# Moving operands kept even columns first and read by TensorE as two halves in turn

## The chip, the core and the metric

The kernel runs on one core of one Trainium2 chip. The metric is the device time of one execution in microseconds (us), smaller being better. The engines of the core are called TensorE (PE, matmuls; PEld, its weight loads), VectorE (DVE), ScalarE (ACT), GpSimd (POOL) and SyncE (SP). SyncE and GpSimd issue the transfers.

## What is computed

One layer on 512 tokens of width 1024: a gated feed-forward block, a token mixer, a second gated block, and a last norm.

```python
for layer in range(DEPTH):                      # DEPTH = 1
    x = x + 0.5 * swiglu(rmsnorm(x, ffn1_norm[layer]), w_gate, w_up, w_down)
    x = x + token_mixer(rmsnorm(x, mix_norm[layer]), w_in, w_out, ...)
    x = x + 0.5 * swiglu(rmsnorm(x, ffn2_norm[layer]), ...)
return rmsnorm(x, final_norm)

def swiglu(x, w_gate, w_up, w_down):            # 1024 -> 2816 -> 1024
    return (silu(x @ w_gate) * (x @ w_up)) @ w_down
```

The mixer projects to queries, keys and values (`h @ w_in`), runs four heads of differential attention (difference of two softmaxes, then a norm) and eight heads of dilated attention in three window configurations, and projects back (`mixed @ w_out`). Everything is float32.

## The kernel before

**Layout.** Activations lie transposed: 128 features on the partitions, the 512 tokens along the free axis. x is eight such tiles of 128 x 512. In most products the weights are the stationary operand (128 x 128) and an activation tile is the moving one, with 512 columns (a whole tile) or 256 (half the tokens, HS = 256).

**Three matmuls for one.** TensorE is fed with the type F32R. Each operand is split in a high part (a cast to F32R, by ScalarE) and a rest (value minus cast, by VectorE), and a product is the sum of three matmuls, in `mm3` (L140 to L143): high weights by high activations, high by rest, rest by high. So there is for each moving operand one cast and one rest: `split_x` (L148) and `early_high`/`early_low` (L1553, L1556) for the inputs of the feed-forward blocks, `activated` (L232) and `kept` (L548, its `cast` L554 and `rest` L557) for the hidden activations, `normed_x` (L257) with `t_sums`, `t_casts`, `t_rests` for the normed x and its sums, `to_mixer` (L882) for the mixer's input, `finish`, `finish_low`, `join` and `mixed_t` for the attention's output.

**The stages.** Each feed-forward block (`ffn`, L216) first does some of its hidden tiles in pairs of gate and up (8 mm3 of 512 columns each, L729), and the rest by a seven-product scheme: two output tiles by two halves of the tokens by the two halves of the inner dimension take seven products instead of eight, on sums and differences of blocks (SEVEN, L46; `product`, L463), 256 columns each, four mm3 per product. The moving operands of a product are picked by `moving` (L426) from the halves of xh/xl or from the sums th/tl. Of the down projection six hidden tiles are done plainly (512 columns, L471), the rest by seven products. The mixer computes queries and keys by mm3 of 512 columns (`qk_chunks`, L1006), scaled copies `scaled` (L1025) bring them from PSUM to SBUF, and values with the activation as the stationary operand and the weights as the moving one (`v_chunks`, L967, L985 to L987). Scores (L1196, L1197), transposes (L1220, L1320) and values by probabilities (L1237, L1339) follow. The output projection does four tiles plainly (`wo_mm`, L1419, 512 columns) and four by seven products (`product`, L1510, from `mixed`).

**Order.** TensorE's order is written out by hand, and from the seventh pair on that of VectorE, ScalarE, SyncE and GpSimd too: events have planned times in ns (STEP and PLAIN_STEP, L56) and ranks, and are issued in that order. The engines then run as their semaphores let them; the planned times themselves set nothing but the order.

**Other streams named later.** `spread` (L208) multiplies ones by a diagonal tile in plain F32 to spread a factor over the partitions (bc_n, 512 columns, L210).

Of the kernel before, what the change touches and what calls it, by code (L numbers as in the profile page):

```python
# [82 lines left out]
def tile_macaron(ctx: ExitStack, tc, xs, xT, wf, wgu1, wst1, wd1, wdg1, wqk, wv, wo, wgu2, wst2, wd2,  # L83
# [15 lines left out]

    def mm_bank(nm):  # L100
        return pp.tile([P, S], F32, tag="mm", name=nm, bufs=4)
# [46 lines left out]
    def split_x(k, norm, h, l, both=False):  # L148
        g = gain(norm, k)
        if both:  # L150
            A.activation(h[:, :256], x[k][:, :256], AF.Copy, scale=g)
            V.tensor_scalar_mul(h[:, 256:], x[k][:, 256:], g)
# [63 lines left out]
    def ffn(wgu, wst, wd, wdg, n0, n1, norm, early, res, nm, hooks, ended, first=None,  # L216
# [15 lines left out]
        def activated(j, t):  # L232
            h = ah[j] = slot(j, f"ah{nm}{j}", F32R)
            l = al[j] = slot(JF + j, f"al{nm}{j}", F32R)
            parts = (lambda: A.copy(h[:], t[:]),
                     lambda: V.tensor_tensor(l[:], t[:], h[:].bitcast(F32), op=ALU.subtract))
# [38 lines left out]
        def t_sums(p, i, q):  # L275

            if not th:
                t_places()
            t0, t1 = nx[2 * p], nx[2 * p + 1]
            u0, u1 = slice(0, HS), slice(HS, S)  # L280
            if i == 0:
                o, a, b = ((t0[:, u0], t0[:, u0], t0[:, u1]), (t0[:, u1], t1[:, u1], t0[:, u1]))[q]
                V.tensor_tensor(o, a, b, op=ALU.subtract)
            else:
                o, a, b = ((t1[:, u1], t1[:, u1], t0[:, u0]), (t1[:, u0], t1[:, u1], t1[:, u0]))[q]
                V.scalar_tensor_tensor(o, a, -1.0, b, op0=ALU.mult, op1=ALU.subtract)

        def t_casts(p, i):
            t = nx[2 * p + i]
            u0, u1 = slice(0, HS), slice(HS, S)  # L290
            if p < 3:
                A.copy(th[p][:, i * S:(i + 1) * S], t[:])
            else:
                for q, u in enumerate((u0, u1)):
                    A.copy(th[p][2 * i + q], t[:, u])

        def t_rests(p, i):
# [4 lines left out]
            else:  # L302
                for q in range(2):
                    V.tensor_tensor(tl[p][:, i * S + q * HS:i * S + (q + 1) * HS],
                                    t[:, q * HS:(q + 1) * HS],
                                    th[p][2 * i + q].bitcast(F32), op=ALU.subtract)
# [119 lines left out]
        def moving(u, block):  # L426
# [7 lines left out]
            c = slice(i * HS, (i + 1) * HS)  # L434
            return [(th[p][i] if p == 3 else th[p][:, c], tl[p][:, c]) for p in range(4)]
# [27 lines left out]
        def product(t):  # L463
            u, o = ops[t]
            h, l = made.pop(t)
            if o[0] == "p":
                m = u[1]
                po = mm_bank(f"pd{nm}{m}")
                for k in range(PLAIN):
                    c = slice(k * P, (k + 1) * P)  # L470
                    mm3(po[:], h[:, c], l[:, c], ah[k][:], al[k][:], k == 0, k == PLAIN - 1)  # L471
# [9 lines left out]
            if t == 0 or ops[t - 1][1][0] == "p":  # L481
                T.matmul(banks[o[1]][:, :P], h[:, :P], moving(u, o[2])[0][0][:, :P],
# [65 lines left out]
        def kept(j, t1, t0, t2):  # L548
# [5 lines left out]
            def cast(o, a):  # L554
                A.copy(o, a)

            def rest(o, a, h):  # L557
                V.tensor_tensor(o, a, h.bitcast(F32), op=ALU.subtract)
# [15 lines left out]
            def b11():  # L574
                t["b"] = places[0]()
                A.copy(t["b"][:, left], g0[:, left])

            def b2():
                t["h2"] = places[1]()
                A.copy(t["h2"][:], g1[:])  # L580
# [5 lines left out]
            def t0_parts():  # L586
                t["h0"] = places[3]()
                A.copy(t["h0"][:], g0[:])
# [5 lines left out]
            def t1_parts():  # L594
                t["h1"] = places[5]()
                A.copy(t["h1"][:], g1[:])

            def t1_rest():
                t["l1"] = places[6]()
                rest(t["l1"][:], g1[:], t["h1"][:])  # L600
                b = hs[j] = {"b11": (t["b"][:, left], t["b"][:, right])}
                for n, i, c in (("b21", 2, left), ("b22", 2, right), ("t1", 0, left),
                                ("t3", 0, right), ("t4", 1, left), ("t2", 1, right)):
                    b[n] = t[f"h{i}"][:, c], t[f"l{i}"][:, c]
# [102 lines left out]
        for j in range(j0, n1):  # L707
# [12 lines left out]
            for hf in range(2):  # L720
# [4 lines left out]
                for kk in range(4):  # L725
                    k = hf * 4 + kk
                    for c, pt in ((0, pg), (1, pu)):
                        o = kk * 256 + c * P
                        mm3(pt[:], wh[:, o:o + P], wl[:, o:o + P], mv[0][k][:], mv[1][k][:],  # L729
                            k == 0, k == KD - 1)  # L730
# [30 lines left out]
    with tc.manual_schedule(engines={mybir.EngineType.DVE, mybir.EngineType.Activation}):  # L761
        for t in range(4):
            raw = wp.tile([P, 1024], F32, tag="raw", name=f"raw_f{t}")
            h, l = w_place()
            for kk in range(2):
# [18 lines left out]
                for j in range(2):  # L784
                    for c in range(2):
                        o = kk * 512 + (2 * j + c) * P
                        mm3(heads[j][c][:], h[:, o:o + P], l[:, o:o + P],
                            early[0][k][:], early[1][k][:], k == 0, k == KD - 1)
# [217 lines left out]
    def qk_chunks(u):  # L1006
# [3 lines left out]
        def chunk(k):  # L1010
# [14 lines left out]
        def scaled():  # L1025
            tq = st["tq"] = slot(28, f"tq{u}")
            tk = st["tk"] = slot(30, f"tk{u}")
            V.scalar_tensor_tensor(tq[:], st["pq"][:], -(HD ** -0.5), held["bc"][:],
                                   op0=ALU.mult, op1=ALU.mult)
            V.tensor_tensor(tk[:], st["pk"][:], held["bc"][:], op=ALU.mult)  # L1030
# [91 lines left out]
    def mixed_t(p):  # L1122
# [3 lines left out]
        n1 = whole["ps"] if p == 3 else t1  # L1126
        u0, u1 = slice(0, HS), slice(HS, S)
# [7 lines left out]
        steps = [lambda: less(t0[:, u0], t0[:, u0], t0[:, u1]),  # L1135
                 lambda: less(t0[:, u1], n1[:, u1], t0[:, u1]),
                 lambda: negative(t1[:, u1], n1[:, u1], t0[:, u0]),
                 lambda: negative(t1[:, u0], t1[:, u1], n1[:, u0])]

        def place():  # L1140
# [8 lines left out]
            b = mixed[p] = {"b11": (mh[2 * p][:, u0], ml[2 * p][:, u0])}  # L1149
            for n, u in (("b21", u0), ("b22", u1)):  # L1150
                b[n] = mh[2 * p + 1][:, u], ml[2 * p + 1][:, u]
            for n, i, u in (("t1", 0, u0), ("t3", 0, u1), ("t4", 1, u0), ("t2", 1, u1)):
                b[n] = o[i][:, u], o[2 + i][:, u]
# [22 lines left out]
    def attention(u, s):  # L1176
# [93 lines left out]
        def finish():  # L1270
# [5 lines left out]
            if diff:  # L1276
                A.activation(h[:], ot[:], AF.Copy, scale=sub8[:])
            else:
                A.copy(h[:], ot[:])
# [571 lines left out]
```

## Time and profile before

| What | Value |
|---|---|
| median of 3 runs | 912.99 us (912.82 to 913.25) |
| span of the profiled execution, first to last instruction | 911.9 us |
| that execution's own time | no other than the span is given; the median is 1.1 us above it |
| TensorE | busy 901.5 us, 6561 matmuls |
| weight loads | busy 844.8 us |
| VectorE, ScalarE, GpSimd | busy 759.5, 546.3, 111.2 us |
| mean granted TensorE clock | 0.996 |
| transfers | 146.86 MB, mean 161 GB/s |

A line such as `L558 DVE TENSOR_TENSOR h2a<-g1a,h1a 128x512 fp32r<-128x512 f32 x8 | 5.5, 684 | 0.0` is read so: source line, engine, operation, the tile written and the tiles read, their shapes and types, how often; then the busy time of the group in us and the mean time of one in ns; then the time that the engine sat idle just before them, and what ended it. TensorE's matmuls are pipelined, so that one's duration (276 ns for 256 columns) is longer than the distance to the next; the pace is read from the distances between starts. The granted clock is a share of TensorE's full speed.

### The profile page before, as it was taken

What the parts mean: (1) busy time and instruction counts of PE and PEld (TensorE: products, weight loads), DVE (VectorE), ACT (ScalarE), POOL (GpSimd) and SP (SyncE); (2) the same over time, 40 slices, a digit from 0 to 9 for tenths busy, and PEclk for the clock granted to TensorE, in tenths of its full rate; (3) what the DMA queues carried; (4) which work ended last, traced back from release to release, by engine and by line L of the source; (5) the groups of instructions that cost most, each with busy time, mean ns of one, the idle gap of its engine ahead of it and who ended that gap; (6) DMA issues with size and microseconds to landing.
All of it is one profiled execution on the core that took longest, in us unless ns stands there. A gap on an engine that the chain in (4) does not pass through costs nothing.

```text
span 911.9 us, 17679 instructions
## 1 busy us (share of the span) xinstructions
PE 901.5 (99%) x6561; PEld 844.8 (93%) x6561; DVE 759.5 (83%) x1603; ACT 546.3 (60%) x1152; POOL 111.2 (12%) x140
## 2 busy tenths in 40 slices
PE   9999999999999999999999999999999999999996
PEld 7889999999999998988989889889999899999995
DVE  7699997687998994788987859999899678799787
ACT  7356674355665764666756848466666354666453
POOL 1001101112203100000000220011110102220100
PEclk9999999999999999999999999999999999999998
DMA  8446756578857742345365674646784757884752
GB/s 276 116 158 155 173 141 179 139 198 216 197 146 198 218 130 92 116 128 152 104 166 146 178 142 110 173 149 154 173 201 107 196 160 180 214 222 122 188 135 93
DMA packets 66374, 146.86 MB, mean 161 GB/s; under 512 B 7680, under 2 KB 9984, under 8 KB 66288
## 3 DMA queue, kind: packets, MB, share of 16 engines
q1 hardware_dynamic: 48672, 113.29, 38.6%
q0 software_dynamic: 17616, 32.45, 21.9%
q8 instruction: 51, 0.84, 0.4%
q14 instruction: 35, 0.29, 0.1%
HBM read 137.28 MB, written 2.14 MB: 153 GB/s over the span
## 4 chain that ended last, share of the span: by engine, by line
PE 95%; DVE 3%; ACT 1%; issue 0%; DMA 0%; DVEq 0%; ACTq 0%
PE po L1237 2%; PE pv L985 2%; PE pv L987 2%; PE pv L986 2%; PE pq L141 1%; PE pq L142 1%; PE pq L143 1%; PE pk L141 1%; PE pk L143 1%; PE pk L142 1%; PE pga L141 1%; PE pga L142 1%; PE pga L143 1%; PE pua L142 1%; PE pua L141 1%; PE pua L143 1%
## 5 line engine op out<-in xcount | busy, mean ns | idle before, releaser
L1202 ACT ACTIVATE pr<-pr,small 128x128 f32<-128x128 f32 (+3 forms) x64 | 35.8, 560 | 30.8 <-DVE small L1199 30.4
L420 ACT CAST w<-s2b 128x512 fp32r<-128x512 f32 x52 | 32.3, 624 | 22.1 <-DVE s2b L402 21.8
L420 ACT CAST w<-s2a 128x512 fp32r<-128x512 f32 x48 | 29.9, 624 | 22.6 <-DVE s2a L402 21.9
L1199 DVE CUSTOM_DVE_ANT_0 pr<-sc,strip 128x128 f32<-128x128 f32 (+3 forms) x64 | 29.7, 486 | 11.5 <-PE sc L1197 11.4
L424 DVE TENSOR_TENSOR w<-s2b,w 128x512 fp32r<-128x512 f32 x52 | 35.7, 686 | 1.7 <-ACT w L420 1.1
L985 PE MATMUL pv<-w,xh 128*128 128x256 f32 x128 | 36.4, 284 | 0.0
L986 PE MATMUL pv<-w,xl 128*128 128x256 f32 x128 | 35.8, 279 | 0.0
L987 PE MATMUL pv<-w,xh 128*128 128x256 f32 x128 | 35.7, 279 | 0.0
L424 DVE TENSOR_TENSOR w<-s2a,w 128x512 fp32r<-128x512 f32 x48 | 32.9, 685 | 1.1 <-ACT w L420 0.7
L141 PE MATMUL pq<-xh,w 128*128 128x512 f32 x64 | 26.9, 421 | 0.0
L920 DVE TENSOR_TENSOR w<-raw_qk,w 128x512 fp32r<-128x512 f32 x32 | 21.6, 685 | 6.1 <-ACT w L916 6.0
L141 PE MATMUL pk<-xh,w 128*128 128x512 f32 x64 | 25.1, 393 | 0.0
L142 PE MATMUL pq<-xl,w 128*128 128x512 f32 x64 | 25.1, 392 | 0.0
L143 PE MATMUL pq<-xh,w 128*128 128x512 f32 x64 | 25.1, 391 | 0.0
L143 PE MATMUL pk<-xh,w 128*128 128x512 f32 x64 | 25.0, 391 | 0.0
L142 PE MATMUL pk<-xl,w 128*128 128x512 f32 x64 | 25.0, 391 | 0.0
L986 PEld LDWEIGHTS pv<-w,xl 128*128 128x128 f32 x128 | 24.1, 189 | 0.1
L985 PEld LDWEIGHTS pv<-w,xh 128*128 128x128 f32 x128 | 24.1, 188 | 0.2
L987 PEld LDWEIGHTS pv<-w,xh 128*128 128x128 f32 x128 | 24.1, 188 | 0.0
L916 ACT CAST w<-raw_qk 128x512 fp32r<-128x512 f32 x32 | 19.3, 616 | 7.4 <-issue 4.4
L1237 PEld LDWEIGHTS po<-v,ptb 128*128 128x128 f32 x160 | 21.6, 191 | 1.6
L1196 PE MATMUL sc<-k,q 128*128 128x256 f32 (+2 forms) x64 | 22.2, 352 | 0.2
(841 smaller groups left out, 4093.3 us busy)
## 6 DMA issues: line engine op xcount, KB each, us to landing
raw_qk<-wqk_dram SPq DMA_DIRECT2D x16, 512.0 KB, 3.7
raw0bg<-wst_dram SPq DMA_DIRECT2D x9, 512.0 KB, 4.3
raw0bu<-wst_dram SPq DMA_DIRECT2D x9, 512.0 KB, 6.0
raw_gua<-wgu_dram SPq DMA_DIRECT2D x8, 512.0 KB, 3.7
raw0ag<-wst_dram SPq DMA_DIRECT2D x8, 512.0 KB, 4.4
raw0au<-wst_dram SPq DMA_DIRECT2D x8, 512.0 KB, 5.3
raw0ad<-wdg_dram SPq DMA_DIRECT2D x8, 512.0 KB, 5.4
strip<-bias_rows SPq DMA_DIRECT2D x16, 256.0 KB, 4.1
```

The lines of the kernel that those rows point to most:

```text
L141: T.matmul(po, wh, mh, start=first, stop=False, skip_group_check=on)
L142: T.matmul(po, wh, ml, start=False, stop=False, skip_group_check=on)
L143: T.matmul(po, wl, mh, start=False, stop=last, skip_group_check=on)
L420: A.copy(made[t][0], source(t))
L424: V.tensor_tensor(l, source(t), h.bitcast(F32), op=ALU.subtract)
L985: T.matmul(po, xh[k][:, xs], wh[:, o:o + 256], start=k == 0, stop=False)
L986: T.matmul(po, xl[k][:, xs], wh[:, o:o + 256], start=False, stop=False)
L987: T.matmul(po, xh[k][:, xs], wl[:, o:o + 256], start=False, stop=k == KD - 1)
L1196: T.matmul(ps[:, :n], qs[:, qi], ks[:, :n], start=True, stop=False)
L1199: V.tensor_tensor_reduce(out=pi, in0=ps[:, :w], in1=st["b"][m][:, w - 1::-1], op0=ALU.add, op1=ALU.min, scale=1.0, scalar=3.0e38, accum_ou ...
L1202: A.activation(pi, pi, AF.Exp, scale=-1.0, bias=st["mx"][:, m, i:i + 1], accum_out=st["ls"][:, m, i:i + 1])
L1237: T.matmul(st["po3"][:, i, d0:d0 + dn], st["ptb", m, i][:, k * P:(k + 1) * P], vk, start=k == 0, stop=k == i)
```

## The change

Helpers for access patterns are added. `evens` reads a row of columns as (even ones, odd ones), that is with a step of two elements; `flat` writes these two halves one behind the other; `full` reads such a tile back in the natural order, column 0 from the first half, column 1 from the second and so on, so its inner dimension has 2 elements, 256 apart for a tile of 512 columns. `part_of` does that for the first or second 256 tokens, `side` names the columns of one half of the tokens without turning them.

```diff
+    def flat(a):
+        return a.rearrange("p (b a) -> p b a", b=2)
+    def evens(a):
+        return a.rearrange("p (a b) -> p b a", b=2)
+    def full(a):
+        return a.rearrange("p (b a) -> p a b", b=2)
+    def part_of(a, i):
+        return a.rearrange("p (b h a) -> p h a b", b=2, h=2)[:, i]
+    def side(a, i):
+        return a.rearrange("p (b h a) -> p h b a", b=2, h=2)[:, i]
...
-            A.activation(h[:], x[k], AF.Copy, scale=g)
-        V.scalar_tensor_tensor(l[:], x[k], g, h[:].bitcast(F32), op0=ALU.mult, op1=ALU.subtract)
+            A.activation(flat(h[:]), evens(x[k]), AF.Copy, scale=g)
+        V.scalar_tensor_tensor(flat(l[:]), evens(x[k]), g, flat(h[:]).bitcast(F32),
+                               op0=ALU.mult, op1=ALU.subtract)
...
-                V.scalar_tensor_tensor(n[:], x[k], gain(norm, k), res["bc"][:],
+                V.scalar_tensor_tensor(flat(n[:]), evens(x[k]), gain(norm, k), evens(res["bc"][:]),
...
             if block[0] == "b":
-                k, c = int(block[1]) - 1, (left, right)[int(block[2]) - 1]
-                return [(xh[2 * p + k][:, c], xl[2 * p + k][:, c]) for p in range(4)]
+                k, c = int(block[1]) - 1, int(block[2]) - 1
+                return [(part_of(xh[2 * p + k][:], c), part_of(xl[2 * p + k][:], c))
+                        for p in range(4)]
...
-                    mm3(po[:], h[:, c], l[:, c], ah[k][:], al[k][:], k == 0, k == PLAIN - 1)
+                    mm3(po[:], h[:, c], l[:, c], full(ah[k][:]), full(al[k][:]),
+                        k == 0, k == PLAIN - 1)
...
             def cast(o, a):
-                A.copy(o, a)
+                A.copy(flat(o), evens(a))
             def rest(o, a, h):
-                V.tensor_tensor(o, a, h.bitcast(F32), op=ALU.subtract)
+                V.tensor_tensor(flat(o), evens(a), flat(h).bitcast(F32), op=ALU.subtract)
...
-                mm3(pt[:], wh[:, o:o + P], wl[:, o:o + P], xh[k][:], xl[k][:],
+                mm3(pt[:], wh[:, o:o + P], wl[:, o:o + P], full(xh[k][:]), full(xl[k][:]),
                     k == 0, k == KD - 1)
...
-            V.tensor_tensor(tk[:], st["pk"][:], held["bc"][:], op=ALU.mult)
+            V.tensor_tensor(flat(tk[:]), evens(st["pk"][:]), flat(held["bc"][:]), op=ALU.mult)
...
-                A.copy(h[:], ot[:])
+                A.copy(flat(h[:]), evens(ot[:]))
```

The same is done in the gate and up pairs, `activated`, `t_sums`, `t_casts`, `t_rests`, `mixed_t`, `finish_whole`, `finish_low`, `join`, `wo_mm`, `early_high` and `early_low`. In the mixer xh and xl stay in the natural order, since `v_chunks` needs them as stationary operands; queries and keys read them by `full` all the same, so their products come out in another order of tokens in PSUM, and `scaled` puts them back by reading PSUM in steps of two. Operations that both read and write tiles in the new order (some sums, casts and rests) go through them in rows as before. The moving operands of scores (k, l), of values (v, tx) and of `v_chunks` (w) are read as before, as are all stationary ones. No instruction, transfer or wait is added or taken away, and the order on each engine is the one before.

More of the change, by code (lines that the diff above doesn't have):

```diff
@@ L278, in t_sums @@
                 t_places()
-            t0, t1 = nx[2 * p], nx[2 * p + 1]
-            u0, u1 = slice(0, HS), slice(HS, S)
+            (a0, a1), (b0, b1) = [[side(nx[2 * p + r][:], c) for c in range(2)] for r in range(2)]
             if i == 0:
-                o, a, b = ((t0[:, u0], t0[:, u0], t0[:, u1]), (t0[:, u1], t1[:, u1], t0[:, u1]))[q]
+                o, a, b = ((a0, a0, a1), (a1, b1, a1))[q]
                 V.tensor_tensor(o, a, b, op=ALU.subtract)
             else:
-                o, a, b = ((t1[:, u1], t1[:, u1], t0[:, u0]), (t1[:, u0], t1[:, u1], t1[:, u0]))[q]
+                o, a, b = ((b1, b1, a0), (b0, b1, b0))[q]
                 V.scalar_tensor_tensor(o, a, -1.0, b, op0=ALU.mult, op1=ALU.subtract)
@@ L289, in t_casts @@
             t = nx[2 * p + i]
-            u0, u1 = slice(0, HS), slice(HS, S)
             if p < 3:
@@ L293, in t_casts @@
             else:
-                for q, u in enumerate((u0, u1)):
-                    A.copy(th[p][2 * i + q], t[:, u])
+                for q in range(2):
+                    A.copy(flat(th[p][2 * i + q]), side(t[:], q))
         def t_rests(p, i):
@@ L430, in moving @@
             if block[0] == "b":
-                k, c = int(block[1]) - 1, (left, right)[int(block[2]) - 1]
-                return [(xh[2 * p + k][:, c], xl[2 * p + k][:, c]) for p in range(4)]
+                k, c = int(block[1]) - 1, int(block[2]) - 1
+                return [(part_of(xh[2 * p + k][:], c), part_of(xl[2 * p + k][:], c))
+                        for p in range(4)]
             i = ("t1", "t3", "t4", "t2").index(block)
-            c = slice(i * HS, (i + 1) * HS)
-            return [(th[p][i] if p == 3 else th[p][:, c], tl[p][:, c]) for p in range(4)]
+            c = slice(i // 2 * S, i // 2 * S + S)
+            mv = [(part_of(th[p][:, c], i % 2), part_of(tl[p][:, c], i % 2)) for p in range(3)]
+            return mv + [(full(th[3][i]), full(tl[3][:, i * HS:(i + 1) * HS]))]
         events, count = [], [0]
@@ L481, in product @@
             if t == 0 or ops[t - 1][1][0] == "p":
-                T.matmul(banks[o[1]][:, :P], h[:, :P], moving(u, o[2])[0][0][:, :P],
+                T.matmul(banks[o[1]][:, :P], h[:, :P], moving(u, o[2])[0][0][:, :P // 2],
                          start=True, stop=False, skip_group_check=True)
@@ L600, in t1_rest @@
                 rest(t["l1"][:], g1[:], t["h1"][:])
[L601 to L604, printed above, removed]
+                b = hs[j] = {"b11": (full(t["b"][:, left]), full(t["b"][:, right]))}
+                for n, i, c in (("b21", 2, 0), ("b22", 2, 1), ("t1", 0, 0),
+                                ("t3", 0, 1), ("t4", 1, 0), ("t2", 1, 1)):
+                    b[n] = part_of(t[f"h{i}"][:], c), part_of(t[f"l{i}"][:], c)
             put(t0 + STEP, b11)
@@ L728, in ffn @@
                         o = kk * 256 + c * P
-                        mm3(pt[:], wh[:, o:o + P], wl[:, o:o + P], mv[0][k][:], mv[1][k][:],
-                            k == 0, k == KD - 1)
+                        mm3(pt[:], wh[:, o:o + P], wl[:, o:o + P], full(mv[0][k][:]),
+                            full(mv[1][k][:]), k == 0, k == KD - 1)
                     if (j, k) in hooks:
@@ L1125, in mixed_t @@
         t0, t1 = whole[2 * p], whole[2 * p + 1]
-        n1 = whole["ps"] if p == 3 else t1
-        u0, u1 = slice(0, HS), slice(HS, S)
+        (a0, a1), (b0, b1) = [[side(t[:], c) for c in range(2)] for t in (t0, t1)]
+        n0, n1 = b0, b1
+        if p == 3:
+            n0, n1 = [evens(whole["ps"][:, c * HS:(c + 1) * HS]) for c in range(2)]
         def less(a, b, c):
@@ L1348, in join @@
             A.copy(t[lo, :], po[hi, :])
-            V.tensor_tensor(whole[u][(lo, hi)[m], :], po[lo, :], t[lo, :], op=ALU.add)
+            V.tensor_tensor(flat(whole[u][(lo, hi)[m], :]), evens(po[lo, :]), evens(t[lo, :]),
+                            op=ALU.add)
         def joined_high():
@@ L1422, in wo_mm @@
             o = k * P
-            mm3(wo_ps[m][:], wh[:, o:o + P], wl[:, o:o + P], mh[k][:], ml[k][:],
+            mm3(wo_ps[m][:], wh[:, o:o + P], wl[:, o:o + P], full(mh[k][:]), full(ml[k][:]),
                 k == 0, k == KD - 1)
@@ L1553, in early_high @@
     def early_high(k):
-        A.activation(early[0][k][:], x[k], AF.Copy, scale=gain(2, k))
+        A.activation(flat(early[0][k][:]), evens(x[k]), AF.Copy, scale=gain(2, k))
     def early_low(k):
-        V.scalar_tensor_tensor(early[1][k][:], x[k], gain(2, k), early[0][k][:].bitcast(F32),
-                               op0=ALU.mult, op1=ALU.subtract)
+        V.scalar_tensor_tensor(flat(early[1][k][:]), evens(x[k]), gain(2, k),
+                               flat(early[0][k][:]).bitcast(F32), op0=ALU.mult, op1=ALU.subtract)
     def add_mixed(m):
```

55 lines of the change are left out of this document (27 added, 28 removed).

## The prediction

> **What bounds the kernel now.** I read the page first: span, busy shares, slices and chain.
>
> ```profile
> span 911.9 us, 17679 instructions
> ...
> PE 901.5 (99%) x6561; PEld 844.8 (93%) x6561; DVE 759.5 (83%) x1603; ACT 546.3 (60%) x1152; POOL 111.2 (12%) x140
> ...
> PEclk9999999999999999999999999999999999999998
> ...
> PE 95%; DVE 3%; ACT 1%; issue 0%; DMA 0%; DVEq 0%; ACTq 0%
> ```
>
> The chain that ended last is TensorE for 95% of the span, at a granted clock of nine tenths or more until the last slice. A busy TensorE can still be one that waits, so I read next what it waited for, in the view of waits for that engine:
>
> ```profile
> PE bcl L1706 <- DVE dgl L1699: 1.6, 1, 1.6
> PE warm L752 <- POOL few L747: 1.0, 1, 1.0
> PE pt L1220 <- DVE tx L1328: 0.2, 1, 0.2
> ```
>
> 2.8 us in all. TensorE is bound by its own rate. The rate is read from the timeline as the distance between starts. The first and the last of 25 matmuls of 512 columns in a row (gate and up, L141 to L143), then of 28 of 256 columns (a seven-product group):
>
> ```profile
> 54.45 0.39 PE L143 MATMUL pga<-eha,w 128*128 128x512 f32 x1
> ...
> 59.89 0.39 PE L143 MATMUL pga<-eha,w 128*128 128x512 f32 x1
> ```
>
> ```profile
> 199.84 0.28 PE L141 MATMUL pzda<-h3a,w 128*128 128x256 f32 x1
> ...
> 202.90 0.28 PE L141 MATMUL pwda<-h1a,w 128*128 128x256 f32 x1
> ```
>
> 24 steps in 5.44 us are 226.7 ns, 27 steps in 3.06 us are 113.3 ns. Half the columns take exactly half the time, so nothing here is a fixed cost of an instruction: it is a price per column, 0.443 ns. Is that the fastest price there is? The trace has other streams beside it, in the chain in order of time (start, us, what, count):
>
> ```profile
> 34.21 0.86 PE bc_n L210 x2
> ...
> 539.81 0.88 PE pt L1220 x8
> ...
> 542.08 1.73 PE po L1237 x16
> ```
>
> bc_n is 512 columns of plain F32 (the program's type there, not F32R), and takes 0.86 / 2 = 430 ns per record. If that is the same stream at half the rate, the whole rate would be 215 ns for 512 columns and 107.5 for 256, not 226.7 and 113.3. So the F32R stream loses one part in nineteen against twice the slow stream, which looks like a bubble of one column time every 18 columns or so. A loss that is strictly per column, that is the same in two stages with different neighbours, and that a stream at half the rate doesn't show, is what a read port at its limit would give. How the port walks through memory is what the change alters.
>
> The other limit near by is the weight load that goes with each matmul: po has only 64 columns (L1237), so its 1.73 / 16 = 108 ns are the load's pace; the transposes (128 columns of F32) go at 0.88 / 8 = 110.
>
> **The change, part by part.**
>
> *The stream.* All matmuls of mm3 (L141 to L143) get a moving operand of [columns/2, 2] with an inner step of 256 elements (128 where a tile holds only one half). From the code, each of the three lines runs 416 times on 512 columns (gate and up in pairs 96 + 64, plain down 96, query and key 128, output projection 32) and 1456 times on 256 (seven products by four tiles by 24 + 26 + 2 units). The view of windows for one of the lines counts the same 1872:
>
> ```profile
> 0.00:912.00 912.00, 569.50 (x1872) 352.06 (x1872) 1.00 0.61 161
> ```
>
> So 1248 matmuls by 226.7 plus 4368 by 113.3 make 282.9 + 494.9 = 778 us of the 912. This is the lever: one ns per 256 columns is worth 4368 + 2 x 1248 = 6.9 us. No moving operand in this trace is read with a step, so the new price is bounded from both sides by the nearest rows. Above: the F32 stream, 430 and 215 ns. Below: half of that, 215 and 107.5, a stream without the bubble. In between lies today's price, if the order does not matter. I take the lower end for 512 columns: there the weight load (108) has twice its time. For 256 columns two limits are then nearly equal, 107.5 for the stream and 108 for the load, and the row nearest to such a pair is the transposes' 110; between 108 and 110 I take 109. The sum: 1248 x (226.7 - 215) = 14.6 us, 4368 x (113.3 - 109) = 18.8 us, together 33.4 us off the path.
>
> The Trainium skill, "TensorE: Matmul & The Clock Gate", section "Back-to-back issue gap", gives N / 2.4 + 2.5 ns for an isolated warm matmul, which is 216 and 109 ns. The rows here say 226.7 and 113.3, so the page and this kernel differ by 4 to 5%, and the measured rows decide for the kernel before. Were its figures what the new order reaches, the sum would be 1248 x 10.7 + 4368 x 4.3 = 32 us, an estimate from that page.
>
> *The strided writes.* No instruction is added. What changes is that the casts, rests and scaled copies that make the operands read every second element, from SBUF or from PSUM, and write two halves. Counted by line over the code they are some 118 VectorE instructions on 512 elements and 19 on 256, and some 81 and 17 on ScalarE. The prices today, with two rows whose inputs do not go forward by one (L1199 reads its strip backwards, L1262 reads f with step 0):
>
> ```profile
> L558 DVE TENSOR_TENSOR h2a<-g1a,h1a 128x512 fp32r<-128x512 f32 x8 | 5.5, 684 | 0.0
> L558 DVE TENSOR_TENSOR h0a<-g0a,h0a 128x256 fp32r<-128x256 f32 x8 | 3.3, 417 | 0.0
> L1199 DVE CUSTOM_DVE_ANT_0 pr<-sc,strip 128x512 f32<-128x512 f32 x16 | 10.6, 685 | 1.5 <-PE sc L1197 1.5
> L1262 DVE TENSOR_TENSOR ob<-po,f 128x512 f32<-128x512 f32 x4 | 2.8, 691 | 0.1
> L580 ACT CAST h1a<-g1a 128x512 fp32r<-128x512 f32 x8 | 5.0, 622 | 9.8 <-DVE g1a L461 9.8
> L576 ACT CAST h0a<-g0a 128x256 fp32r<-128x256 f32 x8 | 3.2, 404 | 1.1 <-DVE g0a L455 1.1
> ```
>
> Backwards and step 0 cost what forwards costs (685 and 691 against 684), so I take nothing for step 2 either. The upper bound is half rate: VectorE pays (684 - 417) / 256 = 1.04 ns an element, so 512 more is 534 ns, and 118 x 0.534 + 19 x 0.267 = 68 us; ScalarE pays 0.85 ns, 39 us in all. A gain is excluded, since the number of elements stays and each already goes one at a time. As long as it is nothing, TensorE's own work hides it; the cover is seen in the view of windows (start:end, length, then PE, PEld, DVE, ACT, POOL busy with counts, clock, DMA share, GB/s):
>
> ```profile
> 30.00:60.00 30.00, 30.00 (x132) 24.47 (x131) 27.71 (x50) 15.37 (x22) 0.00 (x0) 1.00 0.22 72
> 90.00:120.00 30.00, 30.00 (x268) 30.00 (x267) 28.59 (x56) 20.65 (x44) 5.53 (x7) 1.00 0.75 178
> 210.00:240.00 30.00, 30.00 (x267) 30.00 (x267) 24.57 (x46) 20.05 (x43) 7.05 (x8) 1.00 0.86 215
> 300.00:330.00 30.00, 30.00 (x263) 29.91 (x262) 29.96 (x58) 21.67 (x43) 2.31 (x3) 1.00 0.60 168
> 550.00:600.00 50.00, 50.00 (x308) 44.44 (x307) 46.00 (x90) 30.97 (x53) 1.82 (x3) 1.00 0.44 124
> ```
>
> *What is late next.* A TensorE that is 4% faster squeezes the others. VectorE is full in 300 to 330 (29.96 of 30) and 95% full in 90 to 120. Where TensorE would need 28.9 us for what took 30, VectorE still needs 29.96, so about 1 us of the gain is given back there, and I allow 1 us more for bursts in the stages at 92 to 95%. The transfers have room: the highest of these shares, 0.86, becomes 0.89. No wait, queue entry or DMA is added, moved or removed, and the order on each engine is the same.
>
> *The sum.* 33.4 - 2 = 31 us off the profiled execution's 911.9: 881. The median of the runs is 912.99, 1.1 us longer than the span, and I leave that as it is: **882 us**, 3.4% faster. For this likeliest case alone the range runs from 872 (256 columns reach 107.5 too and nothing is given back: 14.6 + 25.3 = 40 us) to 900 (256 columns stay at 113, only the long matmuls gain, and 2 us are given back).
>
> **The rivals.**
>
> *The step halves the stream (slower).* The place is the port that reads the moving operand. If it fetches more than one element at a time and keeps only the last fetch, then every element of an alternating read needs a fetch of its own. For this speaks that today's price is so near a port's limit, and that a half-rate stream exists in the trace. Against it speaks only that bc_n's half rate comes with another type. The price: 1248 x (430 - 226.7) + 4368 x (215 - 113.3) = 254 + 444 = 698 us, time 1611. It decides from the first ns: anything above 113.3 for 256 columns makes the kernel slower, at 6.9 us each. The Trainium skill, "SBUF — State Buffer", section "Door 1: The DMA port swizzle", has a rule that speaks for this rival: lines of 16 bytes, and at least two hits in a row in a line for full bandwidth. By that rule each of the alternating elements lies in another line than the one before, while every second element of a forward read still has two hits in a line, so it would charge TensorE and spare VectorE and ScalarE. No run so far shows it either way for a stepped read.
>
> *The order does not matter.* If the bubble belongs to the F32R type and not to the walk through memory, the streams stay at 113.3 and 226.7. The strided writes are hidden under a TensorE as slow as now, and the time stays at 913. For it: the price is the same in all stages, whatever the tile. Against it: nothing but the argument of the half-rate stream.
>
> *VectorE becomes the bound.* The stream gets faster, but reads of every second element go at half rate. Then VectorE needs 759.5 + 68 = 828 us, and in the stages dense with such writes it passes TensorE: 30 to 60 us has some 13 of them (27.7 + 6.9 = 34.6 against 28.9), 550 to 600 some 16 (46 + 8.5 = 54.5 against 48.2), 90 to 120 some five or six, 2.8 us (31.4 against 28.9). That gives back 5.7 + 6.3 + 2.5 and some 2 in 300 to 330, 16 us: time 898. L1199 and L1262 above speak against it.
>
> **How the numbers follow.** The forecast gets 0.62: the bubble is a fact of the rows, and a per-column loss at the port is more likely to depend on the walk than not. The halved stream gets 0.19, no effect of order 0.12, VectorE as the bound 0.07. A measurement of this kernel can tell about 0.2% from no change, 1.8 us. Of the 0.12 without effect, 0.08 falls within that, 0.03 above it (a few writes late) and 0.01 below. Faster: 0.62 + 0.07 + 0.01 = 0.70; same 0.08; slower 0.19 + 0.03 = 0.22. The range holds the first, third and fourth case, 872 to 915. I widen the lower end by one row of the timeline, in the stage of queries and keys:
>
> ```profile
> 419.83 0.40 PE L141 MATMUL pq<-xh,w 128*128 128x512 f32 x1
> ...
> 420.99 0.39 PE L143 MATMUL pk<-xh,w 128*128 128x512 f32 x1
> ```
>
> Five steps in 1.16 us are 232 ns. If the alternating walk removes these 5.3 ns too, for the 3 x 160 matmuls of that stage and the output projection, that is 2.5 us more, and the lower end is 869. What it leaves out is the halved stream.
>
> **What would show it.** Right: in the stretch of gate and up the distance between starts falls from 226.7 to about 215 ns, in the seven products from 113.3 to about 109; L558 stays at 684 and L580 at 622 ns; the waits of TensorE grow by few us, on VectorE. Wrong in the step of the stream: distances of 113.3 and more. Wrong in the step of the writes: L558 near 1.2 us, or TensorE waiting for casts and rests. If the matmuls of 256 columns stay at 113 while those of 512 fall, the weight load was the limit there.

## The result, and the profile after

The changed kernel takes 898.07 us (median of 4 runs, 897.58 to 898.49) against 913.12 us (912.82 to 913.59) for the kernel before on the same chip: a ratio of 0.9835, 95% interval 0.9821 to 0.9849. It is faster by 15.1 us, or 1.65%, well over the 0.2% that a measurement can tell from no change, and half of the 31 us forecast; 898 lies within the range of 869 to 915.

From the page of the kernel after, its span, busy times and the chain that ended last:

```profile
span 895.8 us, 17678 instructions
...
PE 881.1 (98%) x6561; PEld 837.6 (94%) x6561; DVE 766.8 (86%) x1603; ACT 559.8 (62%) x1152; POOL 111.3 (12%) x140
...
PE 84%; DVE 11%; ACT 2%; issue 2%; DMA 1%; SPq 0%; DVEq 0%; ACTq 0%
```

TensorE's busy time fell by 20.4 us (from 901.5), but the span only by 16.1. VectorE and ScalarE, which got no instruction more, are busy for 7.3 and 13.5 us longer, and VectorE now carries 11% of the chain. What TensorE waits for longest, beside bcl and warm, which wait as long as before (us in total, times, longest):

```profile
PE pga L159 <- DVE w L149: 1.6, 2, 1.1
PE pzda L159 <- DVE w L440: 0.6, 1, 0.6
```

Both are new: matmuls that wait for the rest of a weight tile, late on VectorE. The paces, from the timeline (start, duration), in the same two stretches as before (`mm3` is now at L157 to L159), 21 matmuls of 512 columns and 74 of 256, first and last of each:

```profile
57.27 0.38 PE L157 MATMUL pua<-eha,w 128*128 128x512 f32 x1
...
61.59 0.38 PE L159 MATMUL pua<-eha,w 128*128 128x512 f32 x1
...
193.76 0.28 PE L158 MATMUL pyda<-h2a,w 128*128 128x256 f32 x1
...
201.91 0.28 PE L159 MATMUL pxda<-h5a,w 128*128 128x256 f32 x1
```

20 steps in 4.32 us are 216.0 ns (226.7 before, 215 forecast). 73 steps in 8.15 us are 111.6 ns (113.3 before, 109 forecast). By the counts of the prediction that is 1248 x 10.7 = 13.4 us and 4368 x 1.7 = 7.4 us, together 20.8 us for a forecast of 33.4. The six matmuls of queries and keys that the prediction measured at 232 ns start from 413.06 to 414.13 us now, five steps of about 215 ns.

The instructions that now read every second element, from the view of one tile (durations min/median/max in ns, then first and last start):

```profile
L574 ACT CAST h1a<-g1a x8: 787/819/881, 91.0 to 280.5; 128x512 fp32r<-128x512 f32 x8
L577 DVE TENSOR_TENSOR h2a<-g1a,h1a x8: 720/734/822, 93.3 to 281.5; 128x512 fp32r<-128x512 f32 x8
L280 DVE SCALAR_TENSOR_TENSOR nxa<-x,x,rbc_n x7: 827/937/950, 44.1 to 57.6; 128x512 f32<-128x512 f32 x7
L1047 DVE SCALAR_TENSOR_TENSOR tq<-pq,rbc_n x8: 680/685/692, 353.5 to 510.6; 128x512 f32<-128x512 f32 x8
```

The same view of the kernel before has, for the lines that became L280 and L1047:

```profile
L262 DVE SCALAR_TENSOR_TENSOR nxa<-x,x,rbc_n x7: 741/743/746, 44.8 to 57.1; 128x512 f32<-128x512 f32 x7
L1028 DVE SCALAR_TENSOR_TENSOR tq<-pq,rbc_n x8: 678/684/692, 359.2 to 518.5; 128x512 f32<-128x512 f32 x8
```

Casts went from 622 to 819 ns, rests from 684 to 734, the normed x (two stepped inputs) from 743 to 937. The scaled copy tq, which steps through PSUM, stands at 685 for 684. So the prediction's "nothing" for the stepped reads is wrong, and by an amount that no row of the kernel before showed. Where it reaches TensorE, from the view of windows of the kernel after (columns as before):

```profile
30.00:60.00 30.00, 28.36 (x129) 23.84 (x128) 28.05 (x47) 16.81 (x22) 0.00 (x0) 1.00 0.24 78
270.00:300.00 30.00, 29.42 (x212) 27.71 (x212) 26.48 (x61) 17.80 (x35) 9.84 (x15) 1.00 0.82 205
300.00:330.00 30.00, 29.74 (x265) 29.47 (x265) 29.96 (x60) 22.32 (x45) 1.75 (x2) 1.00 0.56 167
550.00:600.00 50.00, 49.73 (x289) 44.38 (x288) 48.35 (x88) 29.09 (x45) 1.73 (x2) 1.00 0.44 136
```

TensorE has gaps of 1.6, 0.6, 0.3 and 0.3 us in these stretches, where it had none in the three of them that the prediction shows. The largest is at 30 to 60, where eight slow nx (seven of them in the row above, 44.1 to 57.6) stand among the weight rests (w, L149) on VectorE's queue.

### The profile page after: what moved, and what is told of

The parts are those of the page before. It is cut to its first block, busy times and chain, and to the rows that moved or that the text cites. A ratio compares the mean times of both kernels' runs of the same rounds, so it can differ in the third digit from the quotient of the medians.

```text
span 895.8 us, 17678 instructions
## 1 busy us (share of the span) xinstructions
PE 881.1 (98%) x6561; PEld 837.6 (94%) x6561; DVE 766.8 (86%) x1603; ACT 559.8 (62%) x1152; POOL 111.3 (12%) x140
## 4 chain that ended last, share of the span: by engine, by line
PE 84%; DVE 11%; ACT 2%; issue 2%; DMA 1%; SPq 0%; DVEq 0%; ACTq 0%
PE pv L1004 2%; PE pv L1006 2%; PE pv L1005 2%; PE po L1256 2%; PE pdb L157 1%; PE pdb L159 1%; PE pdb L158 1%; PE pq L157 1%; PE pk L157 1%; PE pq L159 1%; PE pk L159 1%; PE pk L158 1%; PE pq L158 1%; DVE w L440 1%; PE pda L157 1%
## 5 line engine op out<-in xcount | busy, mean ns | idle before, releaser
L157 PE MATMUL pq<-xh,w 128*128 128x512 f32 x64 | 26.0, 406 | 0.0
L157 PE MATMUL pk<-xh,w 128*128 128x512 f32 x64 | 24.3, 380 | 0.5 <-DVE ob L1281 0.5
L159 PE MATMUL pk<-xh,w 128*128 128x512 f32 x64 | 24.3, 379 | 0.0
L159 PE MATMUL pq<-xh,w 128*128 128x512 f32 x64 | 24.2, 379 | 0.0
L935 ACT CAST w<-raw_qk 128x512 fp32r<-128x512 f32 x32 | 19.3, 617 | 6.9 <-issue 3.2
```

The source lines that it names most:

```text
L157: T.matmul(po, wh, mh, start=first, stop=False, skip_group_check=on)
L159: T.matmul(po, wl, mh, start=False, stop=last, skip_group_check=on)
```

## The experiments

The theory after the result: the alternating reads gain 20 us, less than forecast because 256 columns meet another limit, and the stepped reads give part of it back. The rivals were that the change's parts are worth what was forecast and something third takes it back, or that the other engines slow TensorE's stream down.

**Only the alternating reads.** TensorE reads two halves in turn, but the operands are written in natural order, so that the tokens stand in another order in these products.

```diff
     def evens(a):
-        return a.rearrange("p (a b) -> p b a", b=2)
+        return a.rearrange("p (b a) -> p b a", b=2)
```

(and the two instructions under `both` in `split_x` read one half of the tile each.)

> The changed kernel with TensorE still reading two halves in turn, but all operands written column after column as before (so the tokens are permuted: only the time counts). Theory: the shortfall is that the matmuls of 256 columns are held by their weight load at about 111.6 ns instead of the 109 forecast; the strided writes gave back little. Then the distances stay at 216 and 111.6 ns, casts and rests return to 622 and 684 ns, and the time is 892 to 896 us. Rival: the slower writes ate most of the gain; then the time falls to about 883.

893.87 us against 913.18, ratio 0.9788 (0.9775 to 0.9801): 19.3 us faster, with casts at 618 and rests at 684 ns. From its view of windows:

```profile
30.00:60.00 30.00, 29.65 (x136) 25.28 (x135) 28.01 (x50) 16.06 (x22) 0.00 (x0) 1.00 0.25 83
270.00:300.00 30.00, 30.00 (x219) 28.45 (x218) 26.71 (x62) 17.29 (x34) 9.76 (x15) 1.00 0.84 215
```

The gaps are 0.35 and 0 us. The reads alone are worth 20.8 us of stream, so 1.5 is given back (2 was forecast). The theory's number is met; the forecast of 883 for the reads without any price of the writes falls.

**Only the stepped reads of ScalarE and VectorE.** The operands are kept even columns first, as in the change, so the instructions that make them read every second element and write two halves, each without gaps. TensorE reads them forwards (tokens again in another order).

```diff
     def full(a):
-        return a.rearrange("p (b a) -> p a b", b=2)
+        return a

     def part_of(a, i):
-        return a.rearrange("p (b h a) -> p h a b", b=2, h=2)[:, i]
+        return a[:, i * HS:(i + 1) * HS]
```

> The changed kernel with the strided writes, but TensorE reading every operand column after column (tokens permuted again: only the time counts). Theory: distances 226.7 and 113.3 ns as before, casts near 815 and rests near 760 ns, time 913 to 916 us, as TensorE at its old pace hides them. Rival (the writes are on the path): 920 us or more.

913.14 us against 913.18, ratio 0.9999 (0.9990 to 1.0008). The time is as expected; the durations, 815 and 760 ns in the expectation, are not. From the view of one tile:

```profile
L574 ACT CAST h1a<-g1a x8: 657/670/687, 92.0 to 284.7; 128x512 fp32r<-128x512 f32 x8
L577 DVE TENSOR_TENSOR h2a<-g1a,h1a x8: 682/684/685, 94.2 to 285.9; 128x512 fp32r<-128x512 f32 x8
```

Casts take 670 ns and not 815, rests 684 and not 760. The same instructions on the same tiles are slow in the one kernel and not in the other; what differs is how TensorE reads. So the loss is neither part's: TensorE's alternating reads alone -19.3 us, the stepped reads alone 0.0, both -15.1. 4.2 us belong to the meeting of the two.

**Streams and reads by themselves.** A kernel that computes nothing of the reference: groups of 24 matmuls back to back, then casts and subtractions without any matmul beside them.

> A kernel that computes nothing of the reference: groups of 24 matmuls in F32R with different walks, column counts and weight widths, then groups of six casts and subtractions. Theory (weight load holds 256 columns): 512 columns 226.7 ns plain and 215 in halves; 256 columns 113.3 plain and 111 to 112 in halves with 128 weight columns, but 107 to 108 in halves with 64 weight columns, where plain stays at 113.3; 64 moving columns with 128 weight columns 108 to 112. Rival (the walk in halves of 256 columns has a price of its own): 111 to 112 with 64 weight columns as well. A distance of 2 elements between the halves, all within 16 bytes, should be like plain if the line matters, like halves if only the order does. Cast from SBUF in steps of two near 815 ns against 622, from PSUM no dearer than plain; subtraction 760 against 684, two stepped inputs about 840.

From the timeline (start, duration, group; plain is forwards, half and part alternate, few has 64 columns of weights, short 64 moving columns, halfd and halfe have halves 16 and 8 bytes apart, steptwo reads every second element; odd puts the weights 13 elements further):

```profile
17.15 5.60 PE L46 MATMUL lplain<-mv,w 128*128 128x512 f32 x24
22.59 5.34 PE L46 MATMUL lhalf<-mv,w 128*128 128x512 f32 x24
27.77 11.00 PE L46 MATMUL lstep<-mv,w 128*128 128x512 f32 x24
38.59 3.06 PE L46 MATMUL plain<-mv,w 128*128 128x256 f32 x24
41.48 2.84 PE L46 MATMUL part<-mv,w 128*128 128x256 f32 x24
44.16 2.92 PE L46 MATMUL plainodd<-mv,w 128*128 128x256 f32 x24
46.91 2.84 PE L46 MATMUL partodd<-mv,w 128*128 128x256 f32 x24
...
54.95 2.96 PE L46 MATMUL plainfew<-mv,w 128*64 128x256 f32 x24
57.75 2.78 PE L46 MATMUL partfew<-mv,w 128*64 128x256 f32 x24
60.37 2.77 PE L46 MATMUL shortplain<-mv,w 128*128 128x64 f32 x24
62.97 2.84 PE L46 MATMUL shorthalf<-mv,w 128*128 128x64 f32 x24
65.65 4.67 PE L46 MATMUL shortodd<-mv,w 128*128 128x64 f32 x24
...
79.51 2.78 PE L46 MATMUL halfd<-mv,w 128*64 128x256 f32 x24
82.13 2.90 PE L46 MATMUL halfe<-mv,w 128*64 128x256 f32 x24
84.87 5.61 PE L46 MATMUL steptwo<-mv,w 128*64 128x256 f32 x24
```

A group's start to the next one's, by 24: 512 columns forwards 226.7 ns, in halves 215.8, every second element 451. 256 columns forwards 120.4 or 114.6 depending on where the weights lie, in halves 111.7. The decisive pair is partfew and shorthalf: with 64 columns of weights the alternating 256 columns take 109.2 ns (107 to 108 expected here, 109 in the prediction); and with 128 columns of weights even 64 moving columns take 111.7. shortplain comes to 108.3 by the same division only because its first step is 31 ns; its other starts lie 111.7 apart too. So 111.7 ns is the pace of a weight load of `mm3`, and it holds the matmuls of 256 columns. halfd against halfe shows how little the walk needs: with 64 columns of weights, forwards takes 116.7 ns (plainfew), 16 bytes apart gains as much as any distance (109.2), and 8 bytes apart a third of that (114.2). shortodd serves only as the end of shorthalf: the granted clock fell to 0.50 in it, at 66.4 us, and was 1.00 in the other groups shown. With no matmul beside them, casts take 618 ns forwards and 659 stepped (815 expected), subtractions 692 and 691 (760 expected).

**The step moved to PSUM.** If it is the stepped reads from SBUF that cost, the order can be undone elsewhere: operands stay in natural order, TensorE reads the two halves of a natural tile in turn, and so its results come out interleaved; whoever takes a result from PSUM reads every second element there and writes two halves. The kernel computes all of the reference. On the kernel before:

```diff
     def mm3(po, wh, wl, mh, ml, first, last, on=False):
+        mh, ml = full(mh), full(ml)
...
-                V.tensor_tensor(t1[:], pg[:], bc[:], op=ALU.mult)
+                V.tensor_tensor(flat(t1[:]), evens(pg[:]), flat(bc[:]), op=ALU.mult)
```

(and so at every other instruction that reads a result of `mm3`, some 30 lines.)

> The kernel before with another way to the same products: all operands stay in the natural order and are written as before, mm3 reads them in two halves in turn, and so the products stand in PSUM with the tokens in another order; whoever brings them from PSUM to SBUF reads every second element there. Nothing is left out. Theory: stepped reads are slowed only in SBUF, where TensorE reads at the same time, and cost nothing from PSUM, so the time is that of the kernel with the reads alone, 892 to 896 us, with casts at 622 and rests at 684 ns. Rival: stepped reads cost in PSUM too, where TensorE writes, and they are more here (about 1.2 reads of PSUM per strided write of the change): 898 to 906 us.

894.36 us against 913.11, ratio 0.9798 (0.9785 to 0.9812), so 3.7 us less than the change: it is the fastest kernel of the study that computes the reference. From its view of one tile, casts and rests cost what they cost before the change:

```profile
L590 ACT CAST h1a<-g1a x8: 614/619/619, 89.0 to 278.0; 128x512 fp32r<-128x512 f32 x8
L568 DVE TENSOR_TENSOR h2a<-g1a,h1a x8: 683/684/686, 91.3 to 279.4; 128x512 fp32r<-128x512 f32 x8
```

**The meeting by itself.** Nothing of the reference: 50 matmuls of 512 columns run beside nine casts or nine subtractions. TensorE reads forwards (plain), in halves 1024 bytes apart (far) or 16 (near); the others read forwards, stepped, or stepped from PSUM.

> A kernel that computes nothing of the reference: stages of 50 matmuls of 512 columns, read plainly, in halves 1024 bytes apart (far) or in halves 16 bytes apart (near), while ScalarE does nine casts or VectorE nine subtractions, plainly, in steps of two from SBUF, or in steps of two from PSUM. Theory (the two kinds of read get in each other's way): casts 618 plain, 660 to 670 in steps beside a plain stream, about 800 in steps beside a far stream, 590 from PSUM beside any; subtractions 690, 690, about 750, 690. Rival (the other engines or the transfers slow them in the kernel): in steps 660 and 690 beside any stream. Without company: 512 columns 226.7 plain, 216 far and near; 256 columns 113 to 114 plain, 111.6 far and near.

Groups by line (busy us, mean ns of one):

```profile
L89 ACT CAST afarstep<-y 128x512 fp32r<-128x512 f32 x9 | 7.7, 861 | 0.3
L89 ACT CAST aplainstep<-y 128x512 fp32r<-128x512 f32 x9 | 5.9, 651 | 0.3
L89 ACT CAST anearstep<-y 128x512 fp32r<-128x512 f32 x9 | 5.8, 650 | 0.3
L89 ACT CAST afarnat<-y 128x512 fp32r<-128x512 f32 x9 | 5.6, 618 | 0.3
L89 ACT CAST afarpsum<-src 128x512 fp32r<-128x512 f32 x9 | 5.3, 586 | 0.3
L91 DVE TENSOR_TENSOR vfarstep<-y,also 128x512 fp32r<-128x512 f32 x9 | 7.3, 813 | 6.2 <-ACT also L82 5.9
L91 DVE TENSOR_TENSOR vnearstep<-y,also 128x512 fp32r<-128x512 f32 x9 | 6.2, 692 | 6.2 <-ACT also L82 5.9
```

One cell of the table stands out on each engine: stepped from SBUF beside far halves, 861 for 650 and 813 for 692 (about 800 and 750 were expected). A forward read beside far halves is not touched (618), nor a stepped one from PSUM (586). TensorE's 50 matmuls take 11.06 us in every alternating stage (about 11.9 forwards, 233 ns a step for the 226.7 expected), whatever runs beside them, so the rival that the others slow its stream falls: it is the others that pay.

**Whose delay is it?** The changed kernel, with the stepped reads of one engine only. High parts and rests then hold the tokens in different orders.

```diff
-            (a line of VectorE)  evens(...)
+            (a line of VectorE)  plain(...)     # "p (b a) -> p b a"
```

(in the first on all lines of VectorE, in the second on all lines of ScalarE.)

> The changed kernel, in which only ScalarE still reads every second element; VectorE reads the same number of elements forwards, so that the high parts of the operands hold the tokens in another order than their rests (the numbers that come out are not the reference's, the instructions are the same). TensorE's reads alternate as in the changed kernel. So far: alternating reads with all writes contiguous 893.9 us, the change 898.1, 4.2 us lost where ScalarE's casts take some 815 ns for 618 and VectorE's rests some 750 for 684. Theory: the loss comes through VectorE, which is nearly full where TensorE waits (28 of 30 us in 30 to 60), and whose work the waits of TensorE name (the rests of weights, w). Then ScalarE's slower casts alone cost little: 894 to 895.5 us, with casts at about 815 ns and rests at 684. Rival: the loss comes through ScalarE, whose late casts hold up the rests of VectorE behind them: 896.5 to 898 us.

> The other half: only VectorE reads every second element, ScalarE reads forwards (again the order of tokens differs between high parts and rests, and nothing else is left out). Theory (the loss comes through VectorE): rests at some 750 ns, casts at 618, and most of the 4.2 us is here: 896.5 to 898 us. Rival (through ScalarE): 894 to 895 us. If both halves come to 894 or 895, it takes the two together; the sum of the two losses against 4.2 us shows whether they add.

Stepped on ScalarE alone: 894.98 us, ratio 0.9800 (0.9787 to 0.9814). On VectorE alone: 896.65 us, ratio 0.9819 (0.9805 to 0.9832). Over the 893.87 of the reads alone that is 1.1 and 2.8 us, 3.9 together for 4.2: they add, within the spread of the runs, and VectorE has the larger part, as the theory had it (1.1 of 0.1 to 1.6 for ScalarE, 2.8 of 2.6 to 4.1 for VectorE). The stretch of 30 to 60 us, first with ScalarE's, then with VectorE's stepped reads:

```profile
30.00:60.00 30.00, 29.65 (x136) 25.29 (x135) 28.01 (x51) 16.88 (x22) 0.00 (x0) 1.00 0.25 81
```

```profile
30.00:60.00 30.00, 28.36 (x129) 23.83 (x128) 28.11 (x46) 15.95 (x22) 0.00 (x0) 1.00 0.22 71
```

TensorE's gap of 1.6 us comes with VectorE's stepped reads and is not there without them.

**How far apart?** As in the meeting by itself, stepped reads only, with TensorE's two places 4 to 512 elements apart (16 to 2048 bytes).

> Computes nothing of the reference: sixteen stages of 50 matmuls of 512 columns, each with nine casts of ScalarE or nine subtractions of VectorE that read every second element of a tile in SBUF. TensorE's moving operand alternates between halves that lie 4, 8, 16, 32, 64, 128, 256 and 512 elements of 4 bytes apart. Known: at 4 (16 bytes) the casts take 650 ns, at 256 (1024 bytes) 861 ns, the subtractions 691 and 813. Theory (something in memory that TensorE's two walks share or not, by distance): there is one distance from which the price jumps, 650 below it and 861 from it on, and the subtractions jump at the same. Rival: it grows step by step with the distance, or depends on what the stepped reader and the matmul happen to meet: 512 elements apart differs again. TensorE's matmuls stay at 216 ns everywhere by both.

Groups by line; the number in a tile's name is the distance in elements:

```profile
L82 ACT CAST a64x<-y 128x512 fp32r<-128x512 f32 x9 | 7.9, 875 | 0.3
L84 DVE TENSOR_TENSOR v64x<-y,also 128x512 fp32r<-128x512 f32 x9 | 7.3, 813 | 6.2 <-ACT also L71 5.9
L84 DVE TENSOR_TENSOR v32x<-y,also 128x512 fp32r<-128x512 f32 x9 | 6.2, 692 | 6.2 <-ACT also L71 5.9
L82 ACT CAST a32x<-y 128x512 fp32r<-128x512 f32 x9 | 6.0, 672 | 0.3
```

There is a jump, and not a slope, between 128 and 256 bytes, on both engines at the same place: 653 to 672 ns up to 128 bytes, 860 to 875 from 256 to 2048; 691 or 692 and 799 to 813 for VectorE. TensorE takes 11.06 us for its 50 matmuls at 8 elements and at 512 alike.

**The jump in the kernel.** The last two are the changed kernel with its stepped reads and writes as they are; only TensorE alternates between other places (tokens come out in another order):

```diff
     def full(a):
-        return a.rearrange("p (b a) -> p a b", b=2)
+        return a.rearrange("p (g b a) -> p g a b", b=2, a=32)   # 64 in the second
```

(`part_of` uses it on its half of the tile.)

> The changed kernel with all its stepped reads and writes as they are; only TensorE's walk is another: it alternates between blocks of 32 elements (128 bytes) within the tile instead of between its halves. The tokens therefore come out in another order (nothing is left out). Theory: the 4.2 us by which the change falls behind the alternating reads alone are the price of stepped reads beside a walk whose two ends lie 256 bytes or more apart; the cost jumps between 128 and 256 bytes. Then here casts take some 670 ns, rests 692 and the time is 894 to 895 us. Rival: the 4.2 us are the stepped reads and writes themselves in the dense stages of the kernel, whatever TensorE's walk: casts at some 815, rests at some 750, 897 to 898.5 us. TensorE's paces are 216 and 111.6 ns by both.

> The same with blocks of 64 elements, so that TensorE alternates between places 256 bytes apart. Theory of the jump: casts at some 815 ns and rests at some 750 again, 897 to 898.5 us, as with the halves 512 or 1024 bytes apart. Rival, if what counts is how far the halves lie apart by degrees, or that they are halves of one tile: between, 895 to 897 us. By both TensorE keeps 216 and 111.6 ns.

128 bytes apart: 893.96 us, ratio 0.9788 (0.9774 to 0.9802). 256 bytes apart: 897.71 us, ratio 0.9830 (0.9816 to 0.9844). The view of one tile, at 128 and at 256 bytes:

```profile
L574 ACT CAST h1a<-g1a x8: 669/682/686, 89.6 to 278.8; 128x512 fp32r<-128x512 f32 x8
L577 DVE TENSOR_TENSOR h2a<-g1a,h1a x8: 681/684/687, 91.8 to 279.9; 128x512 fp32r<-128x512 f32 x8
```

```profile
L574 ACT CAST h1a<-g1a x8: 777/790/875, 91.1 to 280.5; 128x512 fp32r<-128x512 f32 x8
L577 DVE TENSOR_TENSOR h2a<-g1a,h1a x8: 729/734/835, 93.3 to 281.5; 128x512 fp32r<-128x512 f32 x8
```

Both times are the theory's (893.96 at the lower edge of its 894 to 895), and the durations are within about 3% of what it gave; the rival that the stepped reads cost by themselves in the dense stages falls. With every one of them in place, and TensorE's places 128 bytes apart, the kernel is as fast as with none (893.96 and 893.87 us). That settles the 4.2 us.

## Why the prediction had the direction right and the size wrong

**What bounds the kernel: right.** TensorE's own price per column was the lever; changing nothing but the walk of its reads is worth 19.3 us.

**The price of 512 columns: right.** 216.0 ns for the 215 forecast, 13.4 us for 14.6. Half of bc_n's 430 gave the number, though no run shows that the plain F32 stream is free of the bubble for the same reason. The 232 ns of queries and keys fell to the same pace, so that the widening of the range by 2.5 us had a ground, and "the same in all stages" was not quite so before.

**The price of 256 columns: the step that failed most.** The prediction put "107.5 for the stream and 108 for the load" side by side and took 109. The stream's side holds nearly: 109.2 ns where the weights have 64 columns. The load's side doesn't: a weight load of `mm3` takes 111.7. po, whose weights are plain F32, goes no faster, and this was in the trace before. The prediction took its 108 as the chain's time for sixteen matmuls by their number, and not, as it did for the `mm3` streams, as the distance between starts. The third and the last of the same sixteen, from the timeline of the kernel before (start, duration):

```profile
542.09 1.73 PE L1237 MATMUL po<-v,ptb 128*128 128x64 f32 x14
543.54 0.28 PE L1237 MATMUL po<-v,ptb 128*128 128x64 f32 x1
```

13 steps in 1.45 us are 111.5 ns. The first starts at 541.92, so the first two steps take 0.17 us together, and the mean over all fifteen (108) hides the load's pace. With 111.6 in place of 109 the prediction's own sum is 14.6 + 7.4 - 2 = 20.0 us, or 893 us, which is within 1 us of the alternating reads alone (893.87). The term came to 7.4 us for 18.8, and these 11.4 us are the greater part of the miss of 16. The prediction named the sign ("the weight load was the limit there") without giving it a price of its own between 109 and 113. The Trainium skill, "TensorE: Matmul & The Clock Gate", section "LDWEIGHTS (loading the stationary operand)", has P / 1.2, an estimate of 107 ns for 128 columns; the measured 111.7 decides here.

**The stepped reads at nothing: failed by 4.2 us.** By themselves they cost the kernel nothing: 913.14 for 913.18 us (a cast takes 670 ns for 622, which TensorE hides). The rows behind the step, L1199 and L1262, were measured beside a TensorE that reads forwards, and this is the condition that the change takes away; neither of them reads SBUF in steps of two. A price read from before held for the operation and not for its neighbour. The Trainium skill, "SBUF — State Buffer", section "Who interferes with whom", says that TensorE and ScalarE never wait on anyone; the trace agrees for TensorE (50 matmuls in 11.06 us in any company) and not for ScalarE, whose stepped cast goes from 650 to 861 ns by nothing but TensorE's walk.

**The give-back: right in size, only in part where it was put.** It is 1.5 us for 2 by this sum. By the page of the reads alone, TensorE's busy time falls by 21.8 us (879.7 for 901.5) and its idle time grows by 2.0 (12.4 for 10.4). Of that idle time 0.35 us lie at 30 to 60, and 0.26 at 300 to 330 for about 1 that was expected there. The longest of the new waits, 0.5 us of pk for ob (L1281) at 408.7 us, is in the stage of queries and keys, which it didn't name. **From span to median:** every run of the changed kernel takes 1.8 us more than its own span (898.27 and 896.5), and so do runs of the kernel before (913.18 and 911.4). The 1.1 set the median beside the span of another execution, one that with 1.8 us took some 913.7 us (an estimate); this is why 16.1 us lie between the two profiled spans and 15.1 between the medians. The range's 872 left the 1.1 out (913 - 40 = 873), which decides nothing.

**The sum.** 13.4 + 7.4 - 1.5 - 4.2 = 15.1 us, the measured difference. It closes by the way it is made: only 13.4 and 7.4 come from paces, 1.5 and 4.2 are what the times of the reads alone and of the change leave over.

**The rivals.** A halved stream was wrong for the alternating walk: 215.8 ns. A halved stream does exist, for every second element (451 ns). The rule of the Trainium skill that was cited for this rival ("SBUF — State Buffer", section "Door 1: The DMA port swizzle"), 16-byte lines with at least two hits in a row, would charge TensorE and spare the others; measured, TensorE gains from places 16 bytes apart or more (109.2 ns for 116.7) and the others are charged. That the order doesn't matter falls with the reads alone. VectorE as the bound was priced at 898, which is the time that was measured, by another way: that case took 33.4 us from the stream and gave 18 back (the 2 of the sum, and 16 more, which hold the stage at 300 to 330 a second time) through rests slower by 534 ns, and the rests are slower by 50. That the number is met is luck, and an equal sum is not an equal cause; the rows of L577 and the paces tell them apart.

**What stays open.** Why a stepped read and a walk over 256 bytes or more get in each other's way inside the memory, and why the reader pays and not TensorE, no run shows. Of the 3.7 us between the spans of the change and of the reads alone, 2.3 are idle time of TensorE (14.7 for 12.4). The other 1.4 stand as busy time, whose ends are modelled. But the two kernels start the same 6561 matmuls in the same order, and set side by side their starts drift apart at a few places alone: by 1.5 us up to 58 us, 0.8 at 293, 0.3 at 521, 0.4 from 550 to 554 and 0.5 at 592. So nearly all of the 3.7 us is such waits, and no slower stream. In the profile of the change VectorE's rests tta (L317), which read forwards, take 717 ns too (686 before); with TensorE's places 256 bytes apart they take 673, and no run explains the difference.

## What to carry to other kernels

A stream that loses a few per cent per column was freed here by the order in which it is read; ask first what else runs at nearly the same pace (here the weight load, 111.7 ns), and read its pace from the distances between starts behind the first, since the gain ends there. Measure the price of a new access beside the neighbour it will have, by running each part alone and both: parts that cost 0.0 and gain 19.3 gave 15.1. Where a reordered layout has to be paid for, pay on the side that is not disturbed: undone in PSUM it cost 0.5 us over the reads alone (894.36 and 893.87). A walk 128 bytes apart avoids the price too (893.96), but a kernel with writes to match it was not run.

## What the runs showed of the hardware

- TensorE reads F32R forwards at 226.7 ns per 512 columns (233 in another run, whose weights lay elsewhere) and in two places alternately at 215.8. With 64 columns of weights, 256 columns take 116.7 ns forwards, 109.2 in places 16 bytes apart or more and 114.2 in places 8 bytes apart.
- A weight load of 128 columns holds the distance between matmuls at 111.5 to 111.7 ns: F32R in `mm3` (alternating, 256 moving columns) and in shorthalf (64), plain F32 in po (64).
- A forward stream of 256 columns took 120.4 or 114.6 ns with the weights in two different places (one group of 24 each); the alternating one 111.7 in both.
- Stepped reads from SBUF by ScalarE take 861 to 875 ns for 650 to 672, by VectorE 799 to 813 for 692, while TensorE alternates between places 256 bytes or more apart.
- Stepped reads from PSUM cost nothing on either engine (586 ns against 591 forwards on ScalarE; on VectorE 691 against 692 for a forward read of SBUF). Writing alternately into two halves in SBUF is dear: 1102 for 618 ns on ScalarE, 1084 for 692 on VectorE (where one input was read alternately as well).
